# Hybrid encoder on one core: the elementwise work put on DVE alone, weight pieces loaded and stored in another order, and the sample's scores in one tile

## The chip, the cores and the metric

The kernel runs on one core of a Trainium2 chip. The metric is the time of one execution in device microseconds. The engines are PE (matmul; PEld is its weight load), DVE (VectorE), ACT (ScalarE), POOL (GpSimd) and SP (SyncE, which here only issues DMAs).

## The reference

Two layers of a streaming encoder run over 8 tiles of 128 prompt tokens and one tile of 128 sample tokens (8 requests of 16), all in float32, with a model width of 1024. Cut to what matters:

```
h = x @ w_in                                   # 1024 -> 2816, split in 11 parts
yA = sgu(uA, vA, ...) * silu(zA)               # gMLP: layer norm of vA, masked 128x128 mix
f = lb + (1 - lb) * sigmoid(fB); logf = log(f) # HGRN2: chunks of 64, state 64x64 per head
G = cumsum(logf)
A = einsum('bihk,bjhk,bijhk->bhij', q, k, exp(G_i - G_j))          # causal
o = A @ v + (q * exp(G)) @ S
S = exp(GL) * S + (k * exp(GL - G))^T @ v
yB = rmsnorm(o) * norm_b_g * silu(zB)
q, k = rope(qC), rope(kC)                      # first 16 of 64 dims
s = q @ k / 8, window of 128, with a learned sink per head
yC = softmax([s, sink])[..., :-1] @ v * silu(zC)   # sample: keys of the cache and 16 new ones
x = layer_norm(alpha * x + concat(yA, yB, yC) @ w_out)
```

The outputs are the last layer's rows, the new keys and values, and the HGRN states.

## The kernel before

**Groups and units.** The nine tiles are worked in three groups of three, `GROUPS = ((0, 1, 2), (3, 4, "s"), (5, 6, 7))`, for each of two layers: six runs, n = 0 to 5. A run goes through the units of its plan (P0, PN or PL): K, QC, F, Q, IZ, U, Z, C0, C1, V are blocks of columns of `w_in`, O0 and O1 the two halves of `w_out` of the group before. Each is a product over 1024 rows in which both sides are split in a high and a low part: `prod` (L345) makes three matmuls, high by high, low by high and high by low, for each of 8 blocks of rows. Elsewhere a split is a copy of the high part on ACT (L128, the line of the helper `copy`) and a subtraction for the low part (L145, the line of the helper `tt`, which all two-operand elementwise work goes through).

**Lanes.** Between the products PE runs pieces of other work. `tick` advances three lanes by a step: lane C is the attention (`lane_c`, then `attn_sample` for the sample), lane B the recurrence (`lane_b`), lane X the gMLP (`lane_a`). PE's order is the order in which the code is written; the order on the other engines is set by a scheduler with a timeline of its own and priorities, so PE waits where a step of a lane comes up before DVE, ACT or POOL have finished what it reads.

**Lane B.** For each tile `hpre` makes the operands of the recurrence: differences of G (F, with three small ones beside it, and eight pieces X), products of q and k within blocks of four (W), exponentials on ACT, then eight multiplications of X, three of W, and EG = q·exp(G). `lane_b` then fills AQ (masked scores, L727 and L732, and four copies of EG, L756), makes the new state S on DVE (L773), copies S beside the values in vt (`put_state`, L741), multiplies (PE, L822), normalizes (the `pow` of `rstd`, L381, on POOL; then two multiplications, t1b) and transposes (PE, L838).

**Who does the elementwise work.** `POOL_OPS` holds a string for each n; `eng("m")` is POOL if the letter stands in it, else DVE. The letters choose the subtractions of X (m), the small ones of F (g), W (D), rope (r), the low part of x in layer 0 (y), the norm of zb (f), the affine part of the gMLP norm (V), the low part of mix (z), EG (Q), half the multiplications of X (X) and put_state (w). `LNM` chooses for each tile how `out_norm` does its two halves: D is two DVE operations for each half (L899, L904), A replaces the second by ACT and POOL, P both by ACT and two on POOL, S (the last group) does the first half as D and the second as P.

**Weights.** `job(u, j)` brings a piece of 128x512 of unit u. The first time, SP loads it raw (L289) in a ring `wst` of 4, ACT copies the high part in a ring `w` of 11, and DVE or POOL subtracts the low part (DVE for the first `NEA` = 2 units, then in turn). From the fifth unit on ACT stores the high part (L295) and SP the low part (L296) in DRAM, and the other groups of the layer load both from there (L285, SP). `pump` issues jobs while the ring has room.

Of the kernel before, what the change touches and what calls it, by code (L numbers as in the profile page):

```python
# [99 lines left out]
def body(ctx: ExitStack, tc: tile.TileContext, A, O, cst):  # L100
# [172 lines left out]
    ucur = [0]

    def job(u, j):
        l, name, i = wlist[u]
        key = (l, name, i)
        np_ = 4 if name == "w2" else 8
        if j == 0 and key not in kept and u >= NFIRST:
            nm = f"{name}{l}_{i}"  # L280
            kept[key] = u, [dp.tile([P, np_, 512], F32, tag=nm + c, name=nm + c) for c in "hl"]
        src, keep = kept.get(key, (u, None))
        if src < u:
# [123 lines left out]
    def rope(l, t, qk):  # L407
# [5 lines left out]
        tt(eng("r"), a, qk[:, :, 0:16], cb, ALU.mult)  # L413
        tt(eng("r"), b[:, :, 0:8], qk[:, :, 8:16], s0, ALU.mult)
        tt(eng("r"), b[:, :, 8:16], qk[:, :, 0:8], s1, ALU.mult)
        tt(eng("r"), qk[:, :, 0:16], a, b, ALU.add)
# [118 lines left out]
    def attn_sample(l, qk, vd, oT):  # L535
# [22 lines left out]
        dve.tensor_reduce(mxn, psn, AX.X, ALU.max)
        pts, pTs = {}, {}
        NB = 4  # L560
        for k in range(1, NB + 4):
# [25 lines left out]
            if 0 <= k - 1 < NB:  # L587
                p = k - 1
                ps = AXT([P, 2, P])
                for b2 in range(2):  # L590
# [11 lines left out]
                acquire("c4", NC4, *[act.activation(pt[:, b, cs], src, AF.Exp, bias=nM[:, b:b + 1], scale=0.125,  # L602
                                                    accum_out=rs[:, b, q:q + 1])
                                     for b in range(2) for q, cs, src in ((0, slice(0, 128), ps[:, b, :]),
                                                                          (1, slice(128, 144), sn[:, 2 * p + b, :]))])
# [545 lines left out]
```

## Time and profile before

| | before |
|---|---|
| runs | 1135.66, 1129.77, 1135.42 us, median 1135.42 |
| profiled execution | 1132.46 us, of which the span of the instructions is 1130.7 |
| granted TensorE clock, mean | 0.978 of full speed |
| PE busy | 1067.7 us, 94% of the span |
| DVE busy | 647.8 us, 57%, 1666 instructions |
| ACT busy | 517.0 us, 46% |
| POOL busy | 375.9 us, 33%, 506 instructions |

Busy times are those in which an engine executes; register work, waits and the issue of DMAs are not counted. A share of the span is a mean over stretches that differ.

### The profile page before, as it was taken

The numbers are of one execution on the slowest core, as the hardware profiler recorded it, in microseconds if no ns is written. First come the engines' busy times: TensorE is split into PE (matmuls) and PEld (weight loads), VectorE is DVE, ScalarE is ACT, GpSimd is POOL, SyncE is SP. The second block draws the span as 40 slices with busy tenths as digits, with TensorE's granted clock in tenths as the row PEclk, the third lists the DMA queues.
The fourth block names the chain that finished last, engine by engine and source line by source line (L and its number), as shares of the span: only waits on it lengthen the run. The fifth ranks groups of instructions, "written<-read, shape, count | busy, mean of one in ns | idle before, by whom it ended". The sixth has DMA issues, their size and how long they took to land.

```text
span 1130.7 us, 23131 instructions
## 1 busy us (share of the span) xinstructions
PE 1067.7 (94%) x8539; PEld 914.2 (81%) x8539; DVE 647.8 (57%) x1666; ACT 517.0 (46%) x1287; POOL 375.9 (33%) x506
## 2 busy tenths in 40 slices
PE   7969999899999999999999898999999999999986
PEld 5858888787898788898878797977879888888864
DVE  4575775766185365368357668466525626834833
ACT  4487663555332167235257654355443314542210
POOL 4332565242134201476104455232204120213503
PEclk9979999999999999999999999999999999999989
DMA  8656689877757748569876898866946667676533
GB/s 277 234 176 215 233 276 319 285 272 283 245 185 243 267 170 304 192 224 302 291 231 236 317 329 281 280 241 218 318 139 236 225 240 253 205 279 224 179 117 118
DMA packets 143809, 273.11 MB, mean 242 GB/s; under 512 B 16592, under 2 KB 19792, under 8 KB 143696
## 3 DMA queue, kind: packets, MB, share of 16 engines
q1 hardware_dynamic: 125264, 238.07, 62.1%
q10 hardware_dynamic: 18432, 33.56, 8.2%
q8 instruction: 67, 1.10, 0.4%
q14 instruction: 46, 0.38, 0.1%
HBM read 192.93 MB, written 78.64 MB: 240 GB/s over the span
## 4 chain that ended last, share of the span: by engine, by line
PE 65%; DVE 11%; DMA 9%; issue 6%; ACT 5%; POOL 5%; ACTq 0%; SPq 0%; POOLq 0%; DVEq 0%
PE mm L345 50%; DMA wst<-in_w 4%; PE ax L494 2%; PE ax L456 2%; PE ax L485 2%; DVE W L145 1%; POOL X L145 1%; PE ax L570 1%; DVE X L145 1%; ACT w L128 1%; DVE w L145 1%; DMA X<-in_st 1%; DMA wst<-in_wo 1%; POOL w L145 1%; PE ax L855 1%
## 5 line engine op out<-in xcount | busy, mean ns | idle before, releaser
L345 PE MATMUL mm<-w,xh 128*128 128x256 f32 (+1 forms) x1152 | 306.9, 350 | 13.7 <-DVE t3k L376 7.5
L345 PE MATMUL mm<-xh,w 128*128 128x384 f32 x1152 | 313.0, 343 | 0.9 <-DVE tanh L376 0.8
L345 PEld LDWEIGHTS mm<-w,xh 128*128 128x128 f32 x1152 | 205.6, 196 | 45.3 <-DVE t3k L376 8.0
L345 PEld LDWEIGHTS mm<-xh,w 128*128 128x128 f32 x1152 | 212.5, 190 | 4.5 <-ACT t3k L128 1.2
L345 PE MATMUL mm<-w,xl 128*128 128x256 f32 (+1 forms) x576 | 197.7, 345 | 0.0
L345 PE MATMUL mm<-w,mixh 128*128 128x512 f32 x576 | 195.8, 404 | 1.7 <-DMA w<-wo_1h 1.1
L345 PE MATMUL mm<-xl,w 128*128 128x384 f32 x576 | 194.9, 338 | 0.0
L145 POOL TENSOR_TENSOR w<-wst,w 128x512 fp32r<-128x512 f32 x68 | 95.8, 1412 | 163.3 <-ACT w L128 97.5
L345 PEld LDWEIGHTS mm<-w,mixh 128*128 128x128 f32 x576 | 109.0, 189 | 28.1 <-DMA w<-wo_1h 2.2
L345 PEld LDWEIGHTS mm<-w,xl 128*128 128x128 f32 x576 | 112.6, 196 | 10.7
L381 POOL TENSOR_TENSOR sm<-sm,ct 128x4 f32<-128x4 f32 (+2 forms) x42 | 41.7, 992 | 238.6 <-DVE sm L380 238.3
L128 ACT ACTIVATE w<-wst 128x512 fp32r<-128x512 f32 x148 | 91.4, 628 | 61.8 <-DMA wst<-in_w 34.6
L345 PE MATMUL mm<-w,mixl 128*128 128x512 f32 x288 | 112.9, 392 | 0.0
L345 PEld LDWEIGHTS mm<-xl,w 128*128 128x128 f32 x576 | 109.8, 191 | 0.2
L145 DVE TENSOR_TENSOR w<-wst,w 128x512 fp32r<-128x512 f32 x80 | 70.4, 881 | 54.3 <-ACT w L128 50.1
L470 ACT ACTIVATE c<-ax,sm 128x256 f32<-128x256 f32 (+1 forms) x128 | 57.3, 461 | 38.0 <-DVE sm L467 30.6
L145 POOL TENSOR_TENSOR X<-t3k 128x128 f32<-128x128 f32 x136 | 63.1, 498 | 11.2 <-DVE t3k L997 10.3
L345 PEld LDWEIGHTS mm<-w,mixl 128*128 128x128 f32 x288 | 54.7, 190 | 9.8
L456 PE MATMUL ax<-kT,qT 128*128 128x256 f32 (+1 forms) x256 | 42.9, 301 | 10.5 <-DVE qT L145 10.1
L145 POOL TENSOR_TENSOR F<-t3k 128x64 f32<-128x64 f32 (+2 forms) x45 | 20.6, 489 | 90.8 <-DVE t3k L997 47.8
L145 POOL TENSOR_TENSOR t3k<-t3k,ng 128x256 f32<-128x256 f32 x18 | 13.2, 735 | 107.3 <-DVE t3k L376 95.4
L376 DVE SCALAR_TENSOR_TENSOR t3k<-tanh,mm 128x256 f32<-128x256 f32 (+1 forms) x30 | 14.1, 470 | 60.7 <-ACT tanh L374 60.5
(202 smaller groups left out, 1632.7 us busy)
## 6 DMA issues: line engine op xcount, KB each, us to landing
wst<-in_w SPq DMA_DIRECT2D x116, 256.0 KB, 5.1
w<-w_1h SPq DMA_DIRECT2D x44, 256.0 KB, 5.8
w<-w_1l SPq DMA_DIRECT2D x44, 256.0 KB, 5.9
w<-w_0h SPq DMA_DIRECT2D x36, 256.0 KB, 4.9
w<-w_0l SPq DMA_DIRECT2D x36, 256.0 KB, 5.6
xrow<-x SPq DMA_DIRECT2D x18, 512.0 KB, 5.0
wst<-in_wo SPq DMA_DIRECT2D x32, 256.0 KB, 5.1
w<-wo_0h SPq DMA_DIRECT2D x32, 256.0 KB, 5.6
```

Of the source, the lines that this page charges most:

```text
L128: return act.activation(o, i, AF.Copy)
L145: return e.tensor_tensor(o, a, b, op=op)
L345: mm = pe.matmul(out, a(k), b(k), start=n == 0, stop=n == 23)
L376: dve.scalar_tensor_tensor(out, t, 1.0, ps, ALU.add, ALU.mult)
L381: pool.tensor_tensor(out, out, mh[:, :out.shape[-1]], op=ALU.pow)
L456: pe.matmul(ps[:, hh, sl], qT[:, hh, 2 * g + j, :], kk, start=hh + c == 0, stop=False)
L470: acquire("c4", NC4, *[act.activation(pt[:, h, sl], pss[h // 2][:, h % 2, sl], AF.Exp, bias=nM[:, h:h + 1], scale=0.125, accum_out=rs[:, h ...
L485: tr = pe.transpose(ps[:, h, :], pt[:, h, b * P:(b + 1) * P], idn)
L494: mm = pe.matmul(pso[64 * u:64 * u + 64], vv[:, g, :], pT[:, u::2, :], start=first, stop=last)
L570: mm = pe.matmul(pso[64 * u:64 * u + 64, b2, g].rearrange("p r i -> p (r i)"), w[:, 2 * p + b2, 64 * g:64 * g + 64], r[:, 64 * g + 32 * u: ...
L855: pe.matmul(ps[64 * e:64 * e + 64, tl, :], v3[:, tl, gg * 64:(gg + 1) * 64], d["wsS" if m else "wsP"][:, gg, :], start=True, stop=True)
```

## The change

The weight path gets two numbers, `LEAD = 3` (raw pieces issued ahead of the job that uses them) and `LAG = 2` (jobs between a low part and its store). `NEA`, `POOL_OPS`, `LNM` and `eng` go: all of the work named above is on DVE, `put_state` copies on ACT, and `out_norm` is form D for every tile. POOL keeps the 42 `pow` of `rstd`, the memsets and two products of the set-up. In `attn_sample` the scores of the 16 new keys go in the same PSUM tile as those of the 128 cached ones: a tile, a copy, a maximum, a second maximum for each pair, half the exponentials and an addition are gone.

```
-NEA = 2
+LEAD = 3
+LAG = 2
-POOL_OPS = ('mgzfy', 'mDrVyf', 'mgDrzVXQfw', 'mgzf', 'mgDrVyf', 'mgrVQfw')
-LNM = ('DAD', 'DAD', 'DAD', 'DAD', 'DPD', 'SSS')
...
+    raw = [(u, j) for u, j in jobs if u <= kept.get(wlist[u], (u,))[0]]
+    staged, late = [], []
...
+    def ahead(u):
+        while raw and len(staged) < LEAD and raw[0][0] <= u + 1:
+            (l, name, i), j = wlist[raw[0][0]], raw.pop(0)[1]
+            st = T("wst", [P, 512], NWST)
+            acquire("wst", NWST, nc.sync.dma_start(st, A[name][l, i].rearrange("p k c -> p (k c)")[:, 512 * j:512 * j + 512]))
+            staged.append(st)
+
     def job(u, j):
...
+        first, keep = kept.get(wlist[u], (u, None))
+        while late and late[0][0] <= 0:
+            late.pop(0)[1]()
+        for e in late:
+            e[0] -= 1
+        ahead(u)
+        pc = T("w", [P, 2, 512], NPC, F32R)
...
-            st = T("wst", [P, 512], NWST)
-            raw = A[name][l, i].rearrange("p k c -> p (k c)")[:, 512 * j:512 * j + 512]
-            acquire("wst", NWST, nc.sync.dma_start(st, raw))
-            pc = T("w", [P, 2, 512], NPC, F32R)
+            st = staged.pop(0)
             hi = copy(pc[:, 0, :], st)
             acquire("w", NPC, hi)
-            release("wst", tt(dve if u < NEA or j % 2 else pool, pc[:, 1, :], st, pc[:, 0, :].bitcast(F32), ALU.subtract))
-            if keep:
+            release("wst", tt(dve, pc[:, 1, :], st, pc[:, 0, :].bitcast(F32), ALU.subtract))
+            if keep and u == first:
                 nc.scalar.dma_start(keep[0][:, j, :], pc[:, 0, :].bitcast(F32))
-                nc.sync.dma_start(keep[1][:, j, :], pc[:, 1, :].bitcast(F32))
+                late.append([LAG, lambda: nc.sync.dma_start(keep[1][:, j, :], pc[:, 1, :].bitcast(F32))])
...
+        ahead(u)
...
-        psn = AXT([P, 8, 16])
-        for b in range(8):
-            for g in range(2):
-                hp = slice(64 * g, 64 * g + 64)
-                pe.matmul(psn[hp, b, :], qT[hp, b].rearrange("p j i -> p (j i)"), kTn[hp, b * 16:b * 16 + 16],
-                          start=True, stop=True)
-        copy(sn, psn)
-        mxn = T("mxn", [P, 8], 1)
-        dve.tensor_reduce(mxn, psn, AX.X, ALU.max)
...
-                ps = AXT([P, 2, P])
+                ps = AXT([P, 2, 144])
...
+                        pe.matmul(ps[hp, b2, 0:128], q, ck[hp, b, :], start=True, stop=True)
+                        pe.matmul(ps[hp, b2, 128:144], q, kTn[hp, 16 * b:16 * b + 16], start=True, stop=True)
...
-                tt(dve, mx, mx, mxn[:, 2 * p:2 * p + 2], ALU.max)
...
-                tt(eng("o"), pt, pt, rc.unsqueeze(2).to_broadcast([P, 2, 144]), ALU.mult)
+                tt(dve, pt, pt, rc.unsqueeze(2).to_broadcast([P, 2, 144]), ALU.mult)
...
-            xw.append(tt(eng("m"), xv[:, :, :, 0:s], M, gv[:, :, :, 0:s], ALU.subtract))
-            xw.append(tt(eng("m"), xv[:, :, :, s:], gv[:, :, :, s:], M, ALU.subtract))
+            xw.append(tt(dve, xv[:, :, :, 0:s], M, gv[:, :, :, 0:s], ALU.subtract))
+            xw.append(tt(dve, xv[:, :, :, s:], gv[:, :, :, s:], M, ALU.subtract))
...
-                    if "w" in POOL_OPS[cur[0]]:
-                        pool.tensor_copy(dst, sv)
-                    else:
-                        copy(dst, sv)
+                    copy(dst, sv)
...
         for h in range(2):
...
+            z = y[:, 512 * h:512 * h + 512]
+            dve.scalar_tensor_tensor(z, z, mv[:, 0:1], ln[0][h], ALU.subtract, ALU.mult)
+            dve.scalar_tensor_tensor(z, z, mv[:, 2:3], ln[1][h], ALU.mult, ALU.add)
```

All other `eng(...)` became `dve` in the same way.

**DVE in n = 0, at the start of lane B.** The six scans (L997 before, L975 after) make G; what follows is `hpre` of the first tile, with the SiLU of Q's two halves (L376 before, L382 after) and the low parts of weights (w) between. Names carry running numbers, which differ between the two kernels. Before:

```order
L997 SCALAR_TENSOR_TENSOR t3k_460<-mab,t3k_457 128x128 x6
L145 TENSOR_TENSOR F_1083<-t3k_460 128x256
L376 SCALAR_TENSOR_TENSOR t3k_458<-tanh_639,mm_614 128x384
L644 COPY egl_1095<-EG_1084 128x4
L145 TENSOR_TENSOR w_651<-wst_649,w_651 128x512
L145 TENSOR_TENSOR F_1083<-t3k_459,F_1083 128x256
L145 TENSOR_TENSOR w_679<-wst_677,w_679 128x512
L465 TENSOR_REDUCE sm_700<-ax_701 128x2
L376 SCALAR_TENSOR_TENSOR t3k_458<-tanh_697,mm_642 128x384
```

and now:

```order
L144 TENSOR_TENSOR F_1126<-t3k_509 128x64
L144 TENSOR_TENSOR F_1126<-t3k_509 128x64x2
L144 TENSOR_TENSOR F_1126<-t3k_509 128x64x3
L144 TENSOR_TENSOR X_1125<-t3k_509 128x4x32
L382 SCALAR_TENSOR_TENSOR t3k_507<-tanh_688,mm_663 128x384
L144 TENSOR_TENSOR X_1125<-t3k_509 128x4x32
L144 TENSOR_TENSOR X_1125<-t3k_509 128x8x16 x2
L144 TENSOR_TENSOR X_1125<-t3k_509 128x16x8 x2
L144 TENSOR_TENSOR X_1125<-t3k_509 128x32x4
L144 TENSOR_TENSOR w_699<-wst_593,w_699 128x512
```

Between the scans and the first SiLU there was one operation on F and there are now four and one of X; between the two SiLUs (the second is not in the rows shown) there are seven more of X and four low parts of w where there were two. POOL had the rest.

**SP in n = 0, where weights are stored.** `wst` is a raw piece that is loaded, `w_1l` and `w_6l` the places of the low parts in DRAM. Before, the raw pieces in order were 649 (its low part w_651), 664 (w_666), 677, 690, 914; after, 593 (w_699), 606, 619, 703, 716, 729. Before:

```order
L289 DMA wst_677<-in_w 128x512
L296 DMA w_1l<-w_567 128x512
L289 DMA wst_690<-in_w 128x512
L296 DMA w_1l<-w_651 128x512
L289 DMA wst_914<-in_w 128x512
L296 DMA w_6l<-w_679 128x512
```

and now:

```order
L284 DMA wst_703<-in_w 128x512
L304 DMA w_1l<-w_602 128x512
L304 DMA w_1l<-w_615 128x512
L284 DMA wst_716<-in_w 128x512
L304 DMA w_1l<-w_699 128x512
L284 DMA wst_729<-in_w 128x512
L304 DMA w_6l<-w_712 128x512
```

When the low part of raw piece 649 was stored, the three pieces behind it (664, 677, 690) had been issued; now, at the store that belongs to raw piece 593, it is four (606, 619, 703, 716). SP issues 868 DMAs in both kernels.

**DVE at the end.** The last tile's norm; L879, L880 and L887 stand at L869, L870 and L877 now. Before:

```order
L887 BN_AGGR sm_13158<-lst_12954 128x2
L380 TENSOR_SCALAR sm_13158<-sm_13158 128x1
L899 SCALAR_TENSOR_TENSOR xrow_12950<-xrow_12950,sm_13158,t3k_12938 128x512
L891 SCALAR_TENSOR_TENSOR sm_13162<-sm_13158 128x1
L904 SCALAR_TENSOR_TENSOR xrow_12950<-xrow_12950,sm_13158,t3k_12942 128x512
```

and now:

```order
L386 TENSOR_SCALAR sm_13106<-sm_13106 128x1
L881 SCALAR_TENSOR_TENSOR xrow_12904<-xrow_12904,sm_13106,t3k_12892 128x512
L881 SCALAR_TENSOR_TENSOR xrow_12904<-xrow_12904,sm_13106,t3k_12894 128x512
L882 SCALAR_TENSOR_TENSOR xrow_12904<-xrow_12904,sm_13106,t3k_12896 128x512
L882 SCALAR_TENSOR_TENSOR xrow_12904<-xrow_12904,sm_13106,t3k_12898 128x512
```

The second half of the row, which ACT and POOL had, follows the first on DVE; the line for ACT's operand (L891) is gone.

## Rows read from the trace of the kernel before

**Rows 1.** The page, busy time of each engine, share of the span, instructions:
```profile
PE 1067.7 (94%) x8539; PEld 914.2 (81%) x8539; DVE 647.8 (57%) x1666; ACT 517.0 (46%) x1287; POOL 375.9 (33%) x506
```

**Rows 2.** PE's waits: line waited for, us in total, times, longest:
```profile
PE ax L456 <- DVE qT L145: 10.1, 6, 2.4
PE mm L345 <- DVE t3k L376: 7.5, 2, 5.0
PE mm L345 <- ACT w L128: 5.9, 4, 2.8
PE ax L822 <- POOL vt L741: 5.5, 4, 2.6
PE ax L581 <- DVE c L145: 4.5, 2, 2.3
PE ax L838 <- DVE t1b L145: 4.2, 2, 3.3
PE ax L797 <- DMA X<-in_st: 4.2, 2, 2.8
PE ax L822 <- ACT vt L128: 3.3, 2, 1.8
PE ax L822 <- DVE AQ L756: 2.2, 1, 2.2
```

**Rows 3.** POOL's groups: instructions, busy us, mean ns, idle us before:
```profile
L145 POOL TENSOR_TENSOR w<-wst,w 128x512 fp32r<-128x512 f32 x68 | 95.8, 1412 | 163.3 <-ACT w L128 97.5 <-DMA w<-wo_1h 38.8 <-PE mm L345 8.3
L145 POOL TENSOR_TENSOR X<-t3k 128x128 f32<-128x128 f32 x136 | 63.1, 498 | 11.2 <-DVE t3k L997 10.3 <-PE ax L712 0.8
L145 POOL TENSOR_TENSOR xl<-xrow,xh 128x512 fp32r<-128x512 f32 x18 | 23.9, 1336 | 20.8 <-ACT xh L128 19.0 <-DMA xrow<-in_xT 1.7
L145 POOL TENSOR_TENSOR xrow<-xrow,t3k 128x512 f32<-128x512 f32 x18 | 23.8, 1334 | 6.4 <-ACT xrow L895 4.5 <-ACT xrow L901 1.7
L381 POOL TENSOR_TENSOR sm<-sm,ct 128x4 f32<-128x4 f32 (+2 forms) x42 | 41.7, 992 | 238.6 <-DVE sm L380 238.3
```

**Rows 4.** DVE's groups of the same kinds:
```profile
L145 DVE TENSOR_TENSOR w<-wst,w 128x512 fp32r<-128x512 f32 x80 | 70.4, 881 | 54.3 <-ACT w L128 50.1 <-DMA wst<-in_w 3.7
L145 DVE TENSOR_TENSOR X<-X,t3k 128x128 f32<-128x128 f32 x124 | 34.7, 337 | 5.8 <-ACT X L652 5.5
```

**Rows 5.** Windows: us; busy (count) of PE, PEld, DVE, ACT, POOL; clock; DMA share; GB/s:
```profile
500.00:540.00 40.00, 38.76 (x510) 36.32 (x503) 32.58 (x82) 20.84 (x47) 29.11 (x40) 1.00 0.79 264
1040.00:1070.00 30.00, 27.34 (x315) 25.07 (x314) 26.24 (x86) 9.50 (x20) 18.06 (x31) 0.94 0.52 170
```

**Rows 6.** Timeline of lane B in n = 5: start, us, instruction, idle before:
```profile
1057.00 1.85 POOL L145 TENSOR_TENSOR t3k<-t3k,vg 128x768 f32<-128x768 f32 x1
...
1057.26 3.58 DVE L756 COPY AQ<-EG 64x128 f32<-64x128 f32 x2 [0.82 <-ACT AQ L128]
...
1062.21 1.11 POOL L741 COPY vt<-S 64x128 f32<-64x128 f32 x2 [1.46 <-DVE S L773]
...
1063.02 0.85 PE L822 MATMUL ax<-vt,AQ 128*64 128x64 f32 x13 [2.65 <-POOL vt L741]
...
1063.20 0.28 DVE L145 TENSOR_TENSOR X<-X,t3k 128x128 f32<-128x128 f32 x1
```

**Rows 7.** Timeline of n = 0, after the scans:
```profile
67.10 0.69 DVE L145 TENSOR_TENSOR w<-wst,w 128x512 fp32r<-128x512 f32 x1 [0.19 <-ACT w L128]
...
78.00 0.46 DVE L756 COPY AQ<-EG 64x128 f32<-64x128 f32 x2
```

**Rows 8.** Timeline of the sample's attention in layer 0:
```profile
273.21 0.30 ACT L602 ACTIVATE c<-qT,sm 128x16 f32<-128x16 f32 x1
273.40 0.19 ACT L602 ACTIVATION_READ_ACCUMULATOR c<-qT,sm 128x1 f32 x1
```

**Rows 9.** Timeline of the end:
```profile
1124.08 0.75 DVE L904 SCALAR_TENSOR_TENSOR xrow<-xrow,sm,t3k 128x512 f32<-128x512 f32 x1
...
1125.09 2.60 POOL L145 TENSOR_TENSOR xrow<-xrow,t3k 128x512 f32<-128x512 f32 x2 [1.12 <-ACT xrow L895]
```

More of the change, by code (lines that the diff above doesn't have):

```diff
@@ L269, in body @@
     kept = {}
+    for u, key in enumerate(wlist):
+        if u >= NFIRST and key not in kept:
+            nm = f"{key[1]}{key[0]}_{key[2]}"
+            kept[key] = u, [dp.tile([P, 4 if key[1] == "w2" else 8, 512], F32, tag=nm + c, name=nm + c) for c in "hl"]
     units = [([], []) for _ in wlist]
     jobs = [(u, j) for u, (_, name, _) in enumerate(wlist) for j in range(4 if name == "w2" else 8)]
+    raw = [(u, j) for u, j in jobs if u <= kept.get(wlist[u], (u,))[0]]
+    staged, late = [], []
@@ L272, in body @@
     rings["w"] = [0, []]
     ucur = [0]
-    def job(u, j):
[L276 to L283, printed above, removed]
-            pc = T("w", [P, 2, 512], NPC, F32R)
+    def ahead(u):
[4 more added lines that the diff above has]
+            staged.append(st)
@@ L285, in job @@
+    def job(u, j):
+        first, keep = kept.get(wlist[u], (u, None))
[5 more added lines that the diff above has]
+        pc = T("w", [P, 2, 512], NPC, F32R)
+        if first < u:
             acquire("w", NPC, *[nc.sync.dma_start(pc[:, c, :].bitcast(F32), keep[c][:, j, :]) for c in range(2)])
         else:
-            st = T("wst", [P, 512], NWST)
-            raw = A[name][l, i].rearrange("p k c -> p (k c)")[:, 512 * j:512 * j + 512]
@@ L412, in rope @@
         s1 = sinT[:, ti:ti + 1, 8:16].to_broadcast([P, 10, 8])
[L413 to L416, printed above, removed]
+        tt(dve, a, qk[:, :, 0:16], cb, ALU.mult)
+        tt(dve, b[:, :, 0:8], qk[:, :, 8:16], s0, ALU.mult)
+        tt(dve, b[:, :, 8:16], qk[:, :, 0:8], s1, ALU.mult)
+        tt(dve, qk[:, :, 0:16], a, b, ALU.add)
         if t == "s":
@@ L539, in attn_sample @@
         nc.sync.dma_start(vn, vd.rearrange("(b i) c -> i b c", i=16))
-        buf = T("qT", [P, 768], 1)
+        buf = T("qT", [P, 640], 1)
         qT = buf[:, 0:512].rearrange("p (b j i) -> p b j i", b=8, i=16)
-        kTn, sn = buf[:, 512:640], buf[:, 640:768].rearrange("p (b i) -> p b i", i=16)
+        kTn = buf[:, 512:640]
         ps = AXT([P, 4, P])
@@ L588, in attn_sample @@
                 p = k - 1
-                ps = AXT([P, 2, P])
+                ps = AXT([P, 2, 144])
                 for b2 in range(2):
                     for g in range(2):
-                        hp = slice(64 * g, 64 * g + 64)
-                        pe.matmul(ps[hp, b2, :], qT[hp, 2 * p + b2].rearrange("p j i -> p (j i)"),
-                                       ck[hp, 2 * p + b2, :], start=True, stop=True)
+                        hp, b = slice(64 * g, 64 * g + 64), 2 * p + b2
+                        q = qT[hp, b].rearrange("p j i -> p (j i)")
+                        pe.matmul(ps[hp, b2, 0:128], q, ck[hp, b, :], start=True, stop=True)
+                        pe.matmul(ps[hp, b2, 128:144], q, kTn[hp, 16 * b:16 * b + 16], start=True, stop=True)
@@ L595, in attn_sample @@
                 m = T("sm", [P, 20], 12)
-                mx, nM, es, rc = (m[:, 2 * i:2 * i + 2] for i in range(4))
-                rs = m[:, 8:12].rearrange("p (a b) -> p a b", a=2)
+                mx, nM, es, rc, rs = (m[:, 2 * i:2 * i + 2] for i in range(5))
                 dve.tensor_reduce(mx, ps, AX.X, ALU.max)
-                tt(dve, mx, mx, mxn[:, 2 * p:2 * p + 2], ALU.max)
                 dve.tensor_scalar(nM, mx, -0.125, nsinkS[:, l:l + 1], ALU.mult, ALU.min)
                 pt = pts[p] = T("c4", [P, 2, 144], NC4)
[L602 to L605, printed above, removed]
+                acquire("c4", NC4, *[act.activation(pt[:, b, :], ps[:, b, :], AF.Exp, bias=nM[:, b:b + 1], scale=0.125,
+                                                    accum_out=rs[:, b:b + 1]) for b in range(2)])
@@ L660, in hpre @@
                 wv = blk(W4[:, i], 4)[:, :, :, 0:w]
-                tt(eng("F"), wv, wv, E[:, :, :, e0:e0 + w], ALU.mult)
-        tt(eng("Q"), QG, qt, QG, ALU.mult)
+                tt(dve, wv, wv, E[:, :, :, e0:e0 + w], ALU.mult)
+        tt(dve, QG, qt, QG, ALU.mult)
         return X, F, EG, QG, KD
@@ L864, in lane_a @@
             tt(dve, y, ps.rearrange("p t i -> p (t i)"), y, ALU.mult)
-            split(mix[0][:, c, :], mix[1][:, c, :], y, eng("a"))
+            split(mix[0][:, c, :], mix[1][:, c, :], y, dve)
             yield
@@ L881, in ev, with out_norm @@
                 if cb == 1:
-                    out_norm(l, t, ys[tl], sts[tl], LNM[op["n"]][tl], op["ln"])
+                    out_norm(l, t, ys[tl], sts[tl], op["ln"])
             tok_major(w, mix, tl, ev)
-    def out_norm(l, t, y, st, mode, ln):
+    def out_norm(l, t, y, st, ln):
         mv = T("sm", [P, 4], 12)
@@ L888, in out_norm @@
         rstd(mv[:, 2:3], mv[:, 1:2], LN_EPS)
[L889 to L891 removed]
         for h in range(2):
[L893 to L905 removed]
+            z = y[:, 512 * h:512 * h + 512]
+            dve.scalar_tensor_tensor(z, z, mv[:, 0:1], ln[0][h], ALU.subtract, ALU.mult)
+            dve.scalar_tensor_tensor(z, z, mv[:, 2:3], ln[1][h], ALU.mult, ALU.add)
+            if l + 1 == DEPTH:
                 nc.sync.dma_start(yrows(l, t)[:, 512 * h:512 * h + 512], z)
[L907 removed]
+        if l + 1 < DEPTH:
             nc.sync.dma_start(yrows(l, t), y)
@@ L1041, in va @@
                 dve.tensor_scalar(v3[:, tl, :], v3[:, tl, :], mv[:, tl, 0:1], rs[:, tl:tl + 1], ALU.subtract, ALU.mult)
[L1042 to L1043 removed]
+            tt(dve, v3, v3, d["vg"].unsqueeze(1).to_broadcast([P, 3, 256]), ALU.mult)
+            tt(dve, v3, v3, d["vb"].unsqueeze(1).to_broadcast([P, 3, 256]), ALU.add)
             if g == SG:
```

47 lines of the change are left out of this document (12 added, 35 removed).

## Prediction

> **What bounds the kernel now.** The page's busy times come first [rows 1]: PE works 1067.7 of 1130.7 us, so all that a change off PE can win is the 63 us in which PE stands, and the change removes no work from PE worth counting (the scores of the new keys are as many matmuls as before). The waits of PE come next [rows 2]: the nine lines shown sum to 47.4 us. The reader is to see two kinds in them. One kind ends on something that POOL had, or on DVE at a moment when DVE and POOL work side by side: vt from POOL 5.5, t1b 4.2, AQ 2.2, vt from ACT 3.3. The other ends on a chain of its own: qT 10.1 (attention), t3k 7.5 (the scans of n = 0), w 5.9 (the first pieces), c 4.5 (the sample), X from DRAM 4.2. Then the groups of POOL and DVE [rows 3, 4] for what moves, and the windows [rows 5] for where it has to find room. Waits that the profile gives to the engine that came last are read on the timeline [rows 6 to 9].
>
> **The change part by part.** Its own time is 1132.46 us for the profiled execution, 3 us under the median of 1135.42; the three runs lie between 1129.77 and 1135.66.
>
> *What goes to DVE.* The same operation is shorter there: a low part of w takes 1.412 us on POOL [rows 3] and 0.69 on DVE when POOL is idle (67.10 in [rows 7]); a subtraction of X is 0.498 on POOL [rows 3], a DVE multiplication of that shape 0.28 (1063.20 in [rows 6]). The four large groups [rows 3] are 95.8 + 63.1 + 23.9 + 23.8 = 206.6 us on POOL and would be 68 x 0.69 + 136 x 0.28 + 18 x 0.69 + 18 x 0.75 (row 1124.08 of [rows 9]) = 46.9 + 38.1 + 12.4 + 13.5 = 110.9 on DVE, a ratio of 0.54. Of the rest, 375.9 - 206.6 - 41.7 (the pow, which stays) = 127.6 us, at most 69 more come by that ratio; less, since put_state goes to ACT and memsets stay.
>
> *What DVE gets back.* DVE is slower while POOL works. The low part of w means 0.881 on DVE [rows 4] against 0.69, X 0.337 against 0.28, and at the extreme two copies for AQ take 3.58 us beside POOL's 1.85 us product (1057.00 and 1057.26 in [rows 6]), where two copies take 0.46 at 78.00 [rows 7]. For w and X that is 80 x 0.19 + 124 x 0.057 = 22 us, and the other groups have some too. So DVE ends between 647.8 + 111 + 69 - 22 = 806 us and some 740: 65 to 71% of the span.
>
> The Trainium skill says the same of the two engines: "GPSIMD Engine Reference", section 4.1, gives VectorE for elementwise work and calls GPSIMD about twice as slow for two inputs, which the 1.412 against 0.69 agrees with. The same skill also speaks against the change, under the rivals below.
>
> *Where it lands.* In 500 to 540 us DVE is busy 32.6 and POOL 29.1 of 40; in 1040 to 1070 it is 26.2 and 18.1 of 30 [rows 5]. At the ratio of 0.54 that is 48.3 and 36.0, more than the windows hold. If DVE's rows there shrink as w does (0.69 / 0.881 = 0.78), it is 25.4 + 15.7 = 41.1 of 40 and 20.5 + 9.8 = 30.3 of 30. DVE is then about full in the stretches of lane B, with work to either side into which some can slide. That is the open point of the whole forecast: the average leaves room, the hot stretches barely.
>
> *Lane B's waits.* At 1063.02 PE has waited 2.65 us for vt [rows 6]: AQ's slow copies hold DVE until 1060.84, S comes late, and POOL then needs 1.11 us for two copies. With 0.46 in place of 3.58, DVE is 3.1 us earlier, of which the moved X and the affine product of the gMLP norm take part. I count 1.5 there, and at the other places of vt (5.5 + 3.3 in all [rows 2]), AQ (2.2) and t1b (4.2, of which the longest wait, 3.3, has the pow in its chain and stays) 1.5 + 1.0 + 0.5 + 0.5 + 0.3, less 1.0 where DVE fills up: -4.3 of 15.2. Bounds: -15.2 if all end; +10 if DVE is full (the rival below). The clock: in 1040 to 1070 it is granted 0.94 [rows 5], which between full speed (2.4 GHz) and half (1.2) is 0.12 x 30 = 3.6 us at half speed, behind PE's long wait, in which half of the work of that time is lost: if the wait is cut short, -1.7 (0 to -5, for three such places).
>
> *The sample.* Two waits for c of 2.3 us at most [rows 2]. Two of four small exponentials per pair go, each 0.30 + 0.19 us [rows 8], with an addition and a maximum that stood on the same path: about 1.15 in each layer, -2.3, and part of a slow stretch, -0.7: -3.0 (0 to -6).
>
> *The end.* The last half row ended on POOL at 1125.09 + 2.60 = 1127.69 [rows 9]. Now four DVE operations of 0.75 follow each other; the two that wait for the pow start at 1124.08 and end at 1125.6 to 1125.8. The store behind it starts earlier by as much: -1.9 (bounds -1 and -2.1).
>
> *The scans of n = 0.* DVE has three small operations of F and one X ahead of the first SiLU, which PE waits 7.5 us for, together with the second [rows 2]. Three of F at the pace of 0.28 to 0.45 each and an X come to 1 to 1.5 us later, and the X and w behind it also stand ahead of qT: +1.5 (0 to +4).
>
> *Weights, out of the path.* PE waits for w 5.9 us [rows 2], at the very start, where no store is made and the order of loads is unchanged. Later the ring holds 11 pieces, so that loading a raw piece one place earlier on SP, as the order shows, and a store later win nothing on PE: 0 (bounds -2, +2). If this cover went, each late piece would cost PE some 0.7 us. X from DRAM (4.2) does not change. vt on ACT in place of POOL costs ACT a few us of its 54% idle time: 0.
>
> Sum: -4.3 - 1.7 - 3.0 - 1.9 + 1.5 + 0 = -9.4, or 1123 from the profiled execution and 1126 from the median. I take **1125**.
>
> **The rivals.**
>
> *DVE becomes the bound where lane B runs (slower).* One mechanism: in a full stretch a low part or eight subtractions of X stand ahead of the operation that PE waits for, in DVE's single order, where POOL worked on them beside it. For: the windows above, 41.1 of 40 at the better price and 48.3 at the worse. Against: the pieces of `hpre` are for the next tile and can wait for it. Price: the overflow of the two windows is 1.1 to 8.3 and 0.3 to 6.0 us; with four more such stretches (one in each n) at a middle of 3, +18, less the 6.6 that sample, end and clock keep: +11, 1144 to 1147, **1145**. It decides from about 3 us per stretch on.
> The Trainium skill has the rule for it: "Perfetto Trace Analysis", section Optimizing Scalar/DVE Operations, says that where DVE is saturated it may make sense to hand work to ScalarE or even GPSIMD, and adds that the two share an SBUF port, so that it might not help. By its first half 1145 follows, by its second the forecast; the 3.58 us of the AQ copies speaks for the second.
>
> *The gains cancel.* DVE is fuller, so waits for qT (10.1), which lane C takes from the same DVE order, grow by what lane B saves; only end and sample stay, -4.9 + 4, from the median **1134**. For: qT is already the largest wait [rows 2] and the operations ahead of it grow in n = 0.
>
> *All that hangs on POOL ends.* DVE's copies are short throughout: -15.2 - 5 (clock) - 6 - 2.1 = -28, **1104**. Against: DVE's own queue has to stay short at the same time.
>
> *The change does nothing* (DVE's speed not bound by POOL): then the AQ row would be a single case. DVE's means of 0.881 over 80 and 0.337 over 124 speak against it; it falls under the cancelled case.
>
> **How the numbers follow.** Forecast 0.42 (its own range 1116 to 1131), cancelled 0.25, DVE bound 0.21, all of POOL's waits 0.12. The range of 8 in 10 reaches into both outer cases: **1106 to 1146**. A difference under 0.5%, 5.7 us, can't be told from none: under 1129.7 is faster, over 1141.1 slower. Faster: 0.38 of the forecast and all of the last case, 0.50. Same: 0.04 of the forecast, the cancelled case but 0.01, 0.28. Slower: the DVE case and 0.01, 0.22.
>
> **What would show it.** Right: the mean of the w group on DVE near 0.70, of X near 0.28, AQ copies near 0.23 each, DVE busy 740 to 806, POOL under 60; waits for POOL vt gone; the wait for c near 1 us; the last operation on the chain's end on DVE, 3 us before the span's end (1130.7 - 1127.69 is 3.0 now [rows 1, 9]). Wrong: DVE at 0.95 or more in the windows of lane B with PE's waits on AQ, vt or t1b longer than before; more than 12 us of waits on qT; a wait on w after 30 us.

## The result and the profile after

The changed kernel takes 1116.78 us (median of 4 runs, 1113.71 to 1118.10) against 1134.99 (4 runs, 1129.77 to 1135.66): the ratio is 0.985, 95% interval 0.981 to 0.988. That is 18 us faster; 10 were forecast, and the time lies in the range. The profiled execution took 1118.10 us, its span 1116.0.

The page of the changed kernel, busy time of each engine, answers [rows 1]:

```profile
PE 1062.6 (95%) x8539; PEld 912.2 (82%) x8539; DVE 700.6 (63%) x2069; ACT 511.2 (46%) x1264; POOL 49.4 (4%) x57
```

PE stands for 1116.0 - 1062.6 = 53.4 us in place of 63.0, and its matmuls themselves take 5.1 us less. All but 49 of POOL's 376 us went elsewhere, the copies of `put_state` (9.6 us on POOL) to ACT and nearly all the rest to DVE, whose busy time grew by only 53 us.

PE's waits in the changed kernel (line waited for, us in total, times, longest) answer [rows 2]:

```profile
PE ax L812 <- DVE AQ L746: 9.0, 6, 2.5
PE mm L351 <- ACT w L127: 6.9, 4, 3.4
PE mm L351 <- DVE t3k L382: 5.8, 2, 3.4
PE ax L787 <- DMA X<-in_st: 5.5, 2, 3.8
PE ax L462 <- DVE qT L144: 4.3, 4, 1.8
PE ax L828 <- DVE t1b L144: 3.5, 2, 3.3
PE ax L462 <- DVE kT L144: 2.9, 3, 1.8
PE ax L812 <- ACT vt L127: 1.4, 1, 1.4
...
PE ax L578 <- DVE c L144: 0.6, 1, 0.6
```

The reader is to see three things: vt from POOL (5.5) is gone and c fell from 4.5 to 0.6, the attention's qT fell from 10.1 to 4.3, and AQ grew from 2.2 to 9.0. The rival's wait has come, a little smaller than what it replaced (vt from POOL and ACT together fell by 7.4).

DVE's groups of the changed kernel (count, busy us, mean ns, idle before) answer [rows 4]:

```profile
L144 DVE TENSOR_TENSOR w<-wst,w 128x512 fp32r<-128x512 f32 x148 | 100.1, 689 | 35.8 <-ACT w L127 33.3 <-DMA w_0h<-w 1.5
...
L144 DVE TENSOR_TENSOR X<-X,t3k 128x128 f32<-128x128 f32 x136 | 30.9, 294 | 2.8 <-ACT X L645 2.5
L144 DVE TENSOR_TENSOR X<-t3k 128x128 f32<-128x128 f32 x136 | 30.0, 292 | 0.0
...
L746 DVE COPY AQ<-EG 64x128 f32<-64x128 f32 x64 | 14.2, 222 | 2.2 <-ACT AQ L127 0.5
```

The low part of w went from 0.881 to 0.689 us, as priced, and the copies for AQ to 0.222 from the 0.317 of the kernel before:

```profile
L756 DVE COPY AQ<-EG 64x128 f32<-64x128 f32 x64 | 20.3, 317 | 6.8 <-ACT AQ L128 5.3
```

Over all groups that stand in both kernels, before's operations sum to 696 us by their own busy times and to 614 by those of the changed kernel for as many operations (sums over groups, in which time that two groups share in the pipeline counts twice). DVE's work had been longer by 82 us, while what moved adds 167 by the same sum. Three other kernels below that leave POOL idle differ from the changed one by 3 to 4 us in this sum, so smaller differences say nothing.

That POOL is the cause can be read inside the kernel before alone. Of its 80 low parts of w on DVE, the 31 in whose time POOL executes nothing mean 0.688 us, the other 49 mean 1.003. The 64 copies for AQ mean 0.222 (51) and 0.688 (13).

Windows, the changed kernel first (us; busy and count of PE, PEld, DVE, ACT, POOL; clock; DMA share; GB/s), answer [rows 5]; the last row is the kernel before:

```profile
0.00:60.00 60.00, 52.02 (x263) 45.17 (x264) 33.00 (x75) 33.67 (x65) 3.47 (x12) 0.89 0.79 266
500.00:540.00 40.00, 38.43 (x416) 36.07 (x416) 33.09 (x96) 20.93 (x48) 3.18 (x3) 1.00 0.89 305
1030.00:1060.00 30.00, 26.85 (x400) 24.19 (x402) 27.25 (x104) 13.36 (x31) 3.88 (x3) 1.00 0.53 175
...
0.00:60.00 60.00, 52.89 (x268) 45.31 (x269) 29.12 (x58) 31.18 (x56) 22.77 (x26) 0.97 0.79 262
```

Where PE lost in lane B, n = 3, on the timeline of the changed kernel:

```profile
684.87 1.11 DVE L144 TENSOR_TENSOR X<-X,t3k 128x128 f32<-128x128 f32 x5
685.03 0.41 ACT L127 ACTIVATE AQ<-AQ 64x256 f32<-64x256 f32 x1 [0.52 <-DVE AQ L725]
685.88 0.48 DVE L763 SCALAR_TENSOR_TENSOR S<-S,egl,ax 128x64 f32<-128x64 f32 x2
686.26 0.71 DVE L144 TENSOR_TENSOR X<-X,t3k 128x128 f32<-128x128 f32 x3
...
686.86 0.57 DVE L1034 SCALAR_TENSOR_TENSOR oT<-oT,tanh 128x384 f32<-128x384 f32 x1
687.47 0.47 DVE L746 COPY AQ<-EG 64x128 f32<-64x128 f32 x2
...
687.83 0.73 PE L812 MATMUL ax<-vt,AQ 128*64 128x64 f32 x16 [2.54 <-DVE AQ L746]
```

ACT's copy is done at 685.44, and the two copies of 0.47 us that PE needs start at 687.47, behind eight multiplications of X for the next tile, two of S and one of oT: DVE's single order, nothing slow. The multiplications of X are no moved work: in n = 3 they were on DVE before too, where the copies stood between the first five and the other three:

```profile
691.26 1.09 DVE L145 TENSOR_TENSOR X<-X,t3k 128x128 f32<-128x128 f32 x5
692.38 0.47 DVE L756 COPY AQ<-EG 64x128 f32<-64x128 f32 x2
692.88 0.70 DVE L145 TENSOR_TENSOR X<-X,t3k 128x128 f32<-128x128 f32 x3
```

The end, on the timeline of the kernel before (first row) and of the changed one, answers [rows 9]:

```profile
1120.62 0.39 PE L345 MATMUL mm<-w,mixh 128*128 128x512 f32 x1
...
1107.87 0.39 PE L351 MATMUL mm<-w,mixh 128*128 128x512 f32 x1
...
1111.38 1.41 DVE L882 SCALAR_TENSOR_TENSOR xrow<-xrow,sm,t3k 128x512 f32<-128x512 f32 x2
```

From PE's last matmul (1108.26) to the span's end (1115.98) it is 7.7 us; before, 9.7.

### The profile page after: what moved, and what is told of

It is laid out like the page before. It is cut to its first block, busy times and chain, and to the rows that moved or that the text cites. A ratio compares the mean times of both kernels' runs of the same rounds, so it can differ in the third digit from the quotient of the medians.

```text
span 1116.0 us, 22790 instructions
## 1 busy us (share of the span) xinstructions
PE 1062.6 (95%) x8539; PEld 912.2 (82%) x8539; DVE 700.6 (63%) x2069; ACT 511.2 (46%) x1264; POOL 49.4 (4%) x57
## 4 chain that ended last, share of the span: by engine, by line
PE 69%; DVE 13%; DMA 11%; ACT 4%; issue 2%; POOL 0%; ACTq 0%; SPq 0%; DVEq 0%; POOLq 0%
PE mm L351 54%; DVE X L144 2%; PE ax L462 2%; DMA wst<-in_w 2%; PE ax L491 2%; PE ax L500 2%; DVE w L144 1%; PE ax L567 1%; DMA w<-wo_0h 1%; DMA X<-in_st 1%; DVE W L144 1%; DVE F L144 1%; ACT w L127 1%; PE ax L845 1%; PE ax L410 1%
## 5 line engine op out<-in xcount | busy, mean ns | idle before, releaser
L351 PE MATMUL mm<-xh,w 128*128 128x384 f32 x1152 | 309.1, 340 | 0.0
L351 PEld LDWEIGHTS mm<-xh,w 128*128 128x128 f32 x1152 | 209.4, 188 | 3.1 <-ACT t3k L127 0.8
L144 DVE TENSOR_TENSOR w<-wst,w 128x512 fp32r<-128x512 f32 x148 | 100.1, 689 | 35.8 <-ACT w L127 33.3
L351 PEld LDWEIGHTS mm<-w,xl 128*128 128x128 f32 x576 | 112.9, 197 | 10.5
L127 ACT ACTIVATE w<-wst 128x512 fp32r<-128x512 f32 x148 | 91.3, 628 | 49.5 <-DMA wst<-in_w 18.2
L387 POOL TENSOR_TENSOR sm<-sm,ct 128x4 f32<-128x4 f32 (+2 forms) x42 | 43.7, 1040 | 1000.7 <-DVE sm L386 976.4
L869 DVE SCALAR_TENSOR_TENSOR xrow<-xrow,mm 128x512 f32<-128x512 f32 x36 | 24.7, 687 | 45.6 <-PE mm L351 45.0
L127 ACT ACTIVATE pT<-ax 128x512 f32<-128x512 f32 (+1 forms) x76 | 41.0, 550 | 23.2 <-PE ax L491 20.9
L382 DVE SCALAR_TENSOR_TENSOR t3k<-tanh,mm 128x256 f32<-128x256 f32 (+1 forms) x30 | 14.1, 471 | 52.8 <-ACT tanh L380 52.8
L380 ACT ACTIVATE tanh<-mm 128x384 f32<-128x384 f32 (+1 forms) x66 | 30.1, 455 | 35.4 <-PE mm L351 34.2
L462 PEld LDWEIGHTS ax<-kT,qT 128*128 128x128 f32 x256 | 37.2, 198 | 10.5 <-DVE qT L144 5.1
```

Of the source, the lines that this page charges most:

```text
L127: return act.activation(o, i, AF.Copy)
L144: return e.tensor_tensor(o, a, b, op=op)
L351: mm = pe.matmul(out, a(k), b(k), start=n == 0, stop=n == 23)
L380: act.activation(t, ps, AF.Tanh, scale=0.5)
L382: dve.scalar_tensor_tensor(out, t, 1.0, ps, ALU.add, ALU.mult)
L387: pool.tensor_tensor(out, out, mh[:, :out.shape[-1]], op=ALU.pow)
```

## The experiments

Theory A: POOL's work stretches what DVE does at the same time, and was itself twice as long, so the chains through DVE shorten when it stops. Rival B: the order of the weight DMAs did it, since ACT's queue stood for raw pieces. C is the sample. Ratios are to runs of the kernel before on the same chip (medians 1133.8 to 1134.0).

**One part alone.** The kernel before with only the elementwise work moved:

```
-NEA = 2
+NEA = 999
-POOL_OPS = ('mgzfy', 'mDrVyf', 'mgDrzVXQfw', 'mgzf', 'mgDrVyf', 'mgrVQfw')
+POOL_OPS = ('', '', '', '', '', '')
...                       # out_norm and its call as in the changed kernel
```

Expected: 

> The kernel before with only the elementwise work moved: every operation that was on POOL goes to DVE (put_state to ACT), the old order of weight DMAs and the old sample. Theory A (POOL slowed DVE, and its own operations were twice as long, so moving them shortens the chains of lane B): most of the gain of 18 us is here, 1122 to 1126 us, DVE's low part of w near 0.69 us, waits for vt gone. Rival B (the order of the raw pieces is what won: ACT stood for a raw piece with the attention's copies behind it): 1130 to 1133, since only the end (2 us) and little else is left.

Measured: 1119.04 us, ratio 0.988 (0.986 to 0.990). That is 14 us, faster than even A's 1122 to 1126. Two groups of its DVE:

```profile
L145 DVE TENSOR_TENSOR w<-wst,w 128x512 fp32r<-128x512 f32 x148 | 99.9, 687 | 38.0 <-ACT w L128 36.6
...
L756 DVE COPY AQ<-EG 64x128 f32<-64x128 f32 x64 | 14.2, 222 | 2.2 <-ACT AQ L128 0.5
```

They run at the means of the changed kernel with the old DMA order and the old sample, so the durations hang on neither of these.

The kernel before with only the DMA order changed (`LEAD`, `LAG`, `ahead` and `late` as in the diff, low parts still in turn on DVE and POOL):

```
+            release("wst", tt(dve if u < NEA or j % 2 else pool, pc[:, 1, :], st, pc[:, 0, :].bitcast(F32), ALU.subtract))
+                late.append([LAG, lambda: nc.sync.dma_start(keep[1][:, j, :], pc[:, 1, :].bitcast(F32))])
```

Expected: 

> The kernel before with only the order of the weight DMAs changed (raw pieces ahead, low parts stored two jobs later), POOL keeping its work. Theory A: 1133 to 1136, nothing. Rival B: the wait of PE for the SiLU of n = 0 falls from 5.0 to under 3 us and ACT's waits for raw pieces from 47 to about 18 us, 1126 to 1130 us.

Measured: 1139.55 us, ratio 1.006 (1.003 to 1.008), slightly slower. ACT's wait for raw pieces in the kernel before (first row), then this run's and its page:

```profile
ACT w L128 <- DMA wst<-in_w: 34.6, 21, 3.8
...
ACT w L130 <- DMA wst<-in_w: 18.1, 17, 2.9
...
PE mm L357 <- DVE t3k L388: 6.4, 2, 3.6
...
PE 1073.5 (95%) x8539; PEld 920.1 (81%) x8539; DVE 648.0 (57%) x1666; ACT 516.2 (46%) x1287; POOL 373.9 (33%) x506
```

ACT's wait for raw pieces of w_in fell from 34.6 to 18.1 us (with those of w_out from 47.0 to 26.7) and PE's longest for the SiLU of n = 0 from 5.0 to 3.6. That is B's direction, though the second did not get under 3; the time did not fall. Rival B falls. In the profiled run PE's idle time is 59.8 us in place of 63.0 and its busy time 1073.5 in place of 1067.7. The mean granted clock points the same way: 0.961 to 0.972 in its ten runs, against 0.971 to 0.981 in the 21 of before beside them. Why PE was granted less is open.

The kernel before with only the sample changed:

```
...                       # attn_sample as in the changed kernel
-                ps = AXT([P, 2, P])
+                ps = AXT([P, 2, 144])
```

Expected: 

> The kernel before with only the sample's scores in one tile. My term: two waits for c of 2.3 us go to about 1 each or vanish, 1130 to 1132 us (-3 to -5). Rival C (the sample is a larger part than thought, since attention steps behind it come earlier too): 1127 or less.

Measured: 1129.32 us, ratio 0.997 (0.995 to 0.998), 3.6 us. PE's wait for c in it:

```profile
PE ax L572 <- DVE c L145: 0.4, 1, 0.4
```

My term of 3.0, nothing larger; the time lies just under the expected 1130 to 1132.

The changed kernel with the old DMA order (`job` as before, low parts on DVE):

```
-            st = staged.pop(0)
+            st = T("wst", [P, 512], NWST)
+            acquire("wst", NWST, nc.sync.dma_start(st, raw))
...
-                late.append([LAG, lambda: nc.sync.dma_start(keep[1][:, j, :], pc[:, 1, :].bitcast(F32))])
+                nc.sync.dma_start(keep[1][:, j, :], pc[:, 1, :].bitcast(F32))
```

Expected: 

> The changed kernel with the old order of weight DMAs. Theory A: within 2 us of the changed kernel, 1116 to 1119. Rival B: 4 to 6 us lost, 1121 to 1123, of which most before 105 us of the span, with ACT standing for raw pieces in n = 0 again.

Measured: 1116.77 us, ratio 0.985 (0.982 to 0.989): the changed kernel's own time. ACT waits for raw pieces again:

```profile
ACT w L127 <- DMA wst<-in_w: 31.1, 24, 4.8
```

Undone alone, the DMA order costs nothing that the interval of about 4 us either way can show, and 14 + 4 of the two others are the 18. The 6 us that the order alone cost the kernel before do not show here.

**Is it the stretching?** (A1 and A2 split theory A in two.) That DVE's operations are shorter without POOL does not yet show that this made the time. Three kernels give POOL work again. First, every second low part of w goes back to it:

```
-            release("wst", tt(dve, pc[:, 1, :], st, pc[:, 0, :].bitcast(F32), ALU.subtract))
+            release("wst", tt(dve if u < 2 or j % 2 else pool, pc[:, 1, :], st, pc[:, 0, :].bitcast(F32), ALU.subtract))
```

Expected: 

> The changed kernel with every second low part of w (from the third unit on) back on POOL, 68 operations, 47 us off DVE. Theory A1 (POOL's work itself stretches DVE's): DVE's w group goes from 0.689 to over 0.8 us and most of the 47 us is paid back; 1119 to 1125 us. Rival A2 (the gain came only from the moved operations being shorter, and DVE is now full in the stretches of lane B, as its waits of 9 us on AQ say): 1109 to 1114 us.

Measured: 1131.30 us, ratio 0.998 (0.995 to 1.000): 14.5 us over the changed kernel, and slower than A1's 1119 to 1125. Its DVE groups:

```profile
L144 DVE TENSOR_TENSOR w<-wst,w 128x512 fp32r<-128x512 f32 x80 | 66.3, 832 | 29.0 <-ACT w L127 23.0 <-PE ax L677 3.6 <-DMA wo_0l<-w 0.8
...
L746 DVE COPY AQ<-EG 64x128 f32<-64x128 f32 x64 | 17.2, 269 | 2.7 <-ACT AQ L127 1.0
```

DVE is busy 698.3 us although 68 operations left it: at the changed kernel's means 46 us went and, by the sum over all groups, 36 came back as stretch. A1 had the direction and w's mean right, and the cost too small.

Moved work also changes DVE's order, so the second kernel moves none. POOL repeats the same 68 subtractions into the same place:

```
+            lo = tt(dve, pc[:, 1, :], st, pc[:, 0, :].bitcast(F32), ALU.subtract)
+            if u >= 2 and j % 2 == 0:
+                lo = tt(pool, pc[:, 1, :], st, pc[:, 0, :].bitcast(F32), ALU.subtract)
+            release("wst", lo)
```

Expected: 

> The changed kernel in which POOL computes 68 of the low parts of w a second time, into the same place, after DVE has: DVE keeps all of its work, POOL has the same 68 operations of 128x512 as in the run that put them back, and PE has the ring of 11 pieces as cover. Theory A1 (POOL's wide operations stretch DVE's): DVE's summed durations grow by some 30 us, busy from 700 to about 725 to 735, and 1127 to 1136 us. Rival A2 (what cost 14 us there was another order on DVE, or low parts that come late): DVE busy within 5 us of 700 and 1115 to 1120 us.

Measured: 1134.42 us, ratio 1.001 (0.999 to 1.003): the whole gain is gone, with DVE's list unchanged but for its order. Its page:

```profile
PE 1070.8 (95%) x8539; PEld 920.1 (81%) x8539; DVE 734.7 (65%) x2069; ACT 512.1 (45%) x1264; POOL 148.1 (13%) x125
```

and its groups, DVE's and POOL's:

```profile
L144 DVE TENSOR_TENSOR w<-wst,w 128x512 fp32r<-128x512 f32 x148 | 116.4, 799 | 39.6 <-ACT w L127 37.8 <-DMA wo_0l<-w 0.8
...
L144 POOL TENSOR_TENSOR w<-wst,w 128x512 fp32r<-128x512 f32 x68 | 100.1, 1473 | 307.6 <-DVE w L144 185.5 <-DMA w_6h<-w 32.3 <-DMA wst<-in_w 13.4
```

The same 2069 instructions of DVE take 34 us more, and PE's waits on AQ are 12.9 us. A1 holds: 100 us of POOL's work that is of no use make DVE 34 us longer and the kernel 17.6 us. About half of that is PE's idle time (61.9 in place of 53.4 us) and half its busy time (1070.8 in place of 1062.6, at a clock of 0.971 in place of 0.979). POOL also holds each raw piece longer here, and ACT waits more for them than in the changed kernel (18.2 us):

```profile
ACT w L127 <- DMA wst<-in_w: 29.8, 21, 5.2
```

That wait alone need not cost time: with the old DMA order ACT waits 31.1 us and the kernel loses nothing. As in the kernel before, the low parts on DVE split by POOL's work: the 99 without it mean 0.686 us, the 49 beside it 1.028. How much of the 17.6 us is DVE's changed order and not the stretch was not separated. The Trainium skill, "Perfetto Trace Analysis", section Optimizing Scalar/DVE Operations, has the reason as a shared SBUF read port of the two engines; the run agrees with its effect and can't show the port.

The third was to do the same with work that touches nothing:

```
+            if u >= 2 and j % 2 == 0:
+                for _ in range(4):
+                    tt(pool, scr, scr, scr, ALU.mult)   # scr: 128x64
...
+        for _ in range(12):                              # in hpre
+            tt(pool, scr, scr, scr, ALU.mult)
```

Expected: 

> The changed kernel with POOL multiplying a scratch tile that nothing reads: 4 operations of 128x64 at 68 of the weight jobs and 12 in each of the 18 tiles' preparation of lane B. DVE's list is the same but for its order. Theory A1: POOL busy about 230 us, DVE busy up by 15 to 40 us from 700, and 1120 to 1128 us. Rival A2: DVE busy within 5 us of 700 and 1115 to 1119 us (up to 1 us for pow that stands behind the scratch work).

Measured: 1133.22 us, ratio 0.999 (0.997 to 1.002), DVE busy 715.6. The time is beyond A1's 1120 to 1128, and the run doesn't carry A1. The scheduler put all the scratch work before 240 us (the first row is 0 to 100 us, 82.9 busy on POOL; the second 650 to 800, 7.1; busy time of PE, PEld, DVE, ACT, POOL):

```profile
0.00:100.00 100.00, 85.49 (x424) 71.87 (x425) 65.72 (x161) 61.72 (x140) 82.94 (x223) 0.88 0.67 215
...
650.00:800.00 150.00, 142.28 (x1179) 123.96 (x1178) 104.84 (x288) 68.68 (x165) 7.11 (x7) 0.98 0.79 271
```

and there the pow stood behind it, as the timeline shows:

```profile
170.96 7.08 POOL L144 TENSOR_TENSOR scr<-scr 128x64 f32<-128x64 f32 x14
...
178.00 1.01 POOL L392 TENSOR_TENSOR sm<-sm,ct 128x4 f32<-128x4 f32 x1
...
180.15 0.41 PE L835 MATMUL ax<-idn,t1b 128*128 128x128 f32 x2 [3.17 <-DVE t1b L144]
```

What the pow reads was ready on DVE at 174.74. The stretch by the sum over groups is only 10 us. So this kernel shows a second cost, the queue of POOL itself, mixed with the first. The profiled span is 14.5 us longer than the changed kernel's: the work from 71 to 181 us takes 13 us more, with POOL busy for 91 us of it, and that from 665 to 767 takes 6 us more, where POOL is all but idle (4 us). The second is hardly stretch; another order on DVE is the likely cause, which was not shown.

One comparison over all runs bears on this. The four kernels that leave POOL under 50 us of work (the changed one, the moved work alone, the old DMA order, and AQ on ACT below) have different orders on DVE and lie between 1116.8 and 1119.0 us; every kernel that gives POOL 124 us or more lies at 1122 or above.

**Can DVE be relieved?** The subtractions of X back on POOL:

```
-            xw.append(tt(dve, xv[:, :, :, 0:s], M, gv[:, :, :, 0:s], ALU.subtract))
+            xw.append(tt(pool, xv[:, :, :, 0:s], M, gv[:, :, :, 0:s], ALU.subtract))
...                       # and the other half
```

Expected: 

> The changed kernel with the subtractions of X back on POOL in every n, 136 operations, 30 us off DVE. They stand in lane B's own chain (twice as long there, then ACT's exponential). Theory A1: waits for AQ stay or grow, DVE's neighbours (W, AQ, t1b) are stretched, 1119 to 1125 us. Rival A2: the wait for AQ falls under 4 us, 1109 to 1114 us.

Measured: 1122.08 us, ratio 0.989 (0.986 to 0.991), 5 us over the changed kernel. PE's waits on lane B:

```profile
PE ax L812 <- ACT vt L127: 6.0, 4, 2.1
...
PE ax L812 <- DVE AQ L746: 3.7, 2, 3.0
```

A2 was right that AQ falls under 4 us, and wrong on the time: vt is late in its place. Lane B's waits (AQ, vt, t1b) are 13.2 us together, against 13.9 in the changed kernel, so they don't hold the 5 us. DVE stretches little here (11 us by the sum), and a piece of X takes 0.586 us on POOL; where the 5 us arise is open.

The four copies of EG into AQ on ACT:

```
-                    dve.tensor_copy(AQ[o, ch, u::2, :], QG[64 * u:64 * u + 64, :, 64 * ch:64 * ch + 64])
+                    copy(AQ[o, ch, u::2, :], QG[64 * u:64 * u + 64, :, 64 * ch:64 * ch + 64])
```

Expected: 

> The changed kernel with the four copies of EG into AQ (64 in all) on ACT in place of DVE. If DVE's single order is what PE now waits for in lane B (9.0 us in six waits on AQ), most of that goes: 1109 to 1113 us. Rival: ACT then stands in the same chain with vt and the copies, waits move to ACT, 1115 to 1119 us.

Measured: 1116.82 us, ratio 0.983 (0.981 to 0.986), the same as the changed kernel. Its page and its wait on AQ:

```profile
PE 1066.3 (96%) x8539; PEld 915.3 (82%) x8539; DVE 685.5 (61%) x2005; ACT 530.8 (48%) x1328; POOL 48.3 (4%) x57
```

```profile
PE ax L812 <- ACT AQ L127: 2.2, 2, 1.9
```

The waits on AQ fell by 6.8 us and PE's idle time from 53.4 to 48.7; PE's busy time rose by 3.7, at a mean clock of 0.976 in place of 0.979. In this profile the wait taken away came back as slower matmuls, so the rival's time came out by a cause that it didn't name.

**The wide operations alone.** The kernel before with only the low parts of w moved:

```
-NEA = 2
+NEA = 999
```

Expected: 

> The kernel before with only the 68 low parts of w moved from POOL to DVE (96 of POOL's 376 us). If these wide operations carry most of the cost: 1121 to 1127 us, and DVE's mean for w near 0.72. If all of POOL's work costs alike: a quarter of 14 us, 1129 to 1132. If DVE's own load counts for more than the contention: 1134 or slower.

Measured: 1129.79 us, ratio 0.998 (0.995 to 1.000): about 3 us, the figure for "all alike", though the interval reaches 1. DVE's w means 0.752 us. Its group of AQ copies shows why it isn't more:

```profile
L756 DVE COPY AQ<-EG 64x128 f32<-64x128 f32 x64 | 19.8, 310 | 6.3 <-ACT AQ L128 4.5 <-PE ax L822 0.4
```

The rest of POOL's work still stretches what stands in lane B's chain. Taking 68 operations from a POOL that stays busy wins 3 us, giving them to an idle one loses 14.5 to 17.6: the parts don't add.

## Why the prediction was right

The direction and its reason held: POOL's work had made DVE's operations longer and was itself longer there, so moving it shortened what PE waits for. The size is in part luck. 1116.78 us lies at the very edge of the forecast's own 1116 to 1131; what the sum counted on in lane B mostly did not come, and what it had at nothing (qT) or as small (PE's busy time) made up for it. One reading to set right first: the 0.69 us for a low part was taken at 67.10 as a time when POOL is idle, and POOL was at work there, as this row of the kernel before shows. The price is right by the 31 operations above that POOL leaves alone.

```profile
66.46 4.12 POOL L145 TENSOR_TENSOR X<-t3k 128x128 f32<-128x128 f32 x8
```

- **What goes to DVE, and what DVE gets back.** Right in kind: the prices of 0.69 and 0.28 to 0.29 held, and so did the cause. The term that was mis-sized is what DVE gets back. I took 22 us from the two groups whose rows stood side by side and left the rest at "some too"; over all groups it is 82. That is 60 of the 105 us between the upper forecast of 806 and the 700.6 measured; 13 are moved work that was less than thought (167 for 180), and most of the rest is operations that overlap in DVE's pipeline, which my sum of durations counted twice. The hot stretches, which I put at about full (41.1 of 40 and 30.3 of 30), had room: 33.1 and 27.3.
- **Lane B's waits.** I counted -4.3 on the lines of vt, AQ and t1b, 15.2 us together. They are 1.4 + 9.0 + 3.5 = 13.9 now: -1.3. vt fell as expected; AQ took most of it, in DVE's order. "DVE becomes the bound" is thus true of this one place, at 6.8 us, and the run that took those 6.8 us off won no time.
- **qT.** The step that I missed. I took lane C's waits as a chain of its own, and as one that might grow; qT with kT fell from 10.5 to 7.2 us (0.4 for kT before). The subtractions for qT and kT themselves were not shorter (0.689 to 0.688 and 0.286 to 0.287 us). The rope in front of them was: its sum took 0.596 us on POOL and 0.504 on DVE and takes 0.322 now. So were small operations of the softmax on DVE (sm<-sm,nsink from 0.345 to 0.159). That these shortened PE's wait is likely and was not tested alone. With the run that moves only this work at 1119 us, the moved work is worth 14 us where my terms for it sum to -4.3 - 1.7 - 1.9 + 1.5 = -6.4.
- **The scans of n = 0.** Wrong sign: +1.5 forecast, and the line fell from 7.5 to 5.8 us. The four operations do stand ahead of the SiLU now. But the changed kernel with the old DMA order has 7.4 us here and the moved work alone 6.6, so the fall may come from the order of the DMAs; what made it is open.
- **The clock.** -1.7 forecast; PE's busy time fell by 5.1 us for as many matmuls, a third of the 14.7 us between the two profiled spans. The clock came back in the stretch that I named (0.94 in 1040 to 1070 before, 1.00 in 1030 to 1060 now) and was lost at the start (0.97 to 0.89 in the first 60 us), so its mean only went from 0.978 to 0.979. What else made PE's busy time shorter was not taken apart.
- **The sample.** -3.0 forecast, 3.6 measured alone, c from 4.5 to 0.6.
- **The end.** -1.9 forecast, 2.0 measured.
- **Weights.** 0 forecast, 0 (within about 4 us) measured with the rest in place; -2 to +2 was too narrow for the order alone, which cost the kernel before 6 us.

## What to carry to other kernels

Before work is shared out between VectorE and GpSimd, compare the mean of the same operation of VectorE where GpSimd works and where it is idle, for every group and not for the two largest: here the stretch over all was half of what the shared-out work would have cost on VectorE. Such work is worth testing by doubling it uselessly on GpSimd, which keeps the other engine's list as it is, if not its order. And read PE's busy time beside its idle time: a wait that was removed here (AQ on ACT) came back as slower matmuls.

## What the runs showed of the hardware that was not expected

POOL's operations do not all stretch DVE alike. By the sum over groups, DVE grew by 31 us for 100 us of 128x512 subtractions on POOL (36 for 103 in the run that moved them), by 11 for 75 us of 128x128 ones on X, and by 10 for 189 us of 128x64 multiplications of one tile with itself: about 0.3, 0.15 and 0.05 us per us, the last two from differences not far above the 3 to 4 us that this sum can't tell apart. Whether the width, the operands or the place in the program makes the difference was not taken apart.

Nor are all of DVE's operations stretched. Of its groups that stand in both kernels, 25 read a PSUM tile (ax or mm), and none of them was more than 0.006 us longer before than now, though many ran beside POOL: of the 64 predicated copies AQ<-ct,ax, the 50 with POOL at work mean 0.219 us and the 14 others 0.218. The whole stretch lies in groups that read SBUF alone: w, AQ<-EG, X, W, t1b and the small sm among them. One such group of the attention, before and now:

```profile
L145 DVE TENSOR_TENSOR qT<-ax,qT 64x512 fp32r<-64x512 f32 x32 | 22.0, 689 | 11.7 <-ACT qT L128 11.1
...
L144 DVE TENSOR_TENSOR qT<-ax,qT 64x512 fp32r<-64x512 f32 x32 | 22.0, 688 | 9.0 <-ACT qT L127 8.5
```

And with the change of DMA order alone the granted clock was lower in all ten runs than before's mean (mean 0.968 against 0.975), for a cause that stays open.
